# Down projection of a hybrid decoder layer: nine rooms for raw operands in place of five

## The chip, the cores and the metric

The kernel runs on one core of a Trainium2 chip. The metric is the device time of one execution in microseconds, as the median of several runs. Before the change it is 2085.34 us (three runs, 2084.3 to 2087.26). Smaller is better.

## The reference

One layer of a decoder trunk is computed for a prompt of 1024 tokens and for 8 single sampled tokens, 1032 columns in all, in float32. The layer has a gated delta rule, a sliding-window attention, an output projection and a gated feed-forward part with a short causal convolution; a final norm ends it. What matters here is its end:

```
h2 = _rmsnorm(x, lp['norm2_w']) * (1 + sc2) + sh2
gate = h2 @ lp['w_ffn_gate']
up = h2 @ lp['w_ffn_up']
...
gc = _causal_dwconv(gate_ext, lp['ffn_conv_w'], L) + lp['ffn_conv_b']
x = x + gt2 * ((jax.nn.silu(gc) * up) @ lp['w_ffn_down'])
```

The model width is 1024 and the hidden width D_FF is 2816, which is 22 tiles of 128 (`FT`).

## The kernel before

**Precision.** Each float32 operand is split in two parts, a high part that ACT (ScalarE) writes as a rounded copy and a low part that DVE (VectorE) forms as the difference (`split`, lines 127 to 130). A product is three matmuls, high by high, high by low and low by high (`mm3`, lines 178 to 182). So nearly all TensorE work carries line 180, 181 or 182, and all splits line 129 (ACT) and line 130 (DVE).

**Seven products for eight.** Gate, up and down each use a scheme of Winograd's kind: operands are cut in halves along two dimensions, sums and differences of the halves are formed, and seven half-size products give the four quarters of the result. Gate and up are computed for pairs of hidden tiles (`ffn_gate_up`, 11 passes); their weights are combined on POOL (GpSimd, line 1589) and split into tiles with the tags w0 to w6, of which w0 to w3 lie in the pool `pw`. At the end of each pass the seven combinations of the hidden activations go to a DRAM scratch, `xd` (lines 1718 to 1721): two directly, five after sums on POOL.

**The down projection** is `ffn_down`, from line 1726. Its seven products are called `i` = 5, 3, 4, 7, 1, 2, 6 in that order, grouped in chains `(5, 3)`, `(4, 7)`, `(1,)`, `(2,)`, `(6,)`. Each product sums over `G` = 11 tiles, so there are 77 steps `s`. A step has three stages:

- `fetch(s)` (line 1742) loads 128 columns by 512 of the weight on SP's DMA queue (line 1751) and 128 by 516 of activations from `xd` (line 1756) into one raw room of 1028 elements per partition. For the products 3, 4, 7, 1 and 6 the weight is a sum or difference of two blocks; the second block goes to a tile `ws` with three buffers (line 1754), and POOL combines the two (line 1755).
- `part(s)` (line 1759) splits the room: ACT writes the high half, DVE the low half, into an operand room. There are 13 operand rooms, taken in turn by the list `tags` (line 1730), so the operands of step s take the place of those of step s - 13. An `issue_after` keeps later splits behind certain instructions, among them `self.took`, the last copy of `take` (line 1763).
- `step(s, ...)` (line 1775) issues 24 matmuls, three for each of 8 PSUM banks: two column halves by four blocks of 128 output rows.

After a product's last step, `take` (line 1783) copies each of its 8 banks to SBUF on ACT (line 1786, tile `bml`). Inside a chain the next product goes on adding to the same banks, so its first matmul into a bank waits for that bank's copy. The copies are then added to the result by `add_gated` on DVE, two a step (lines 1472, 1476 and 1477). The last product, 6, is done bank by bank with the final norm between (`norm_rows`).

**The raw rooms before.** They are five, chosen by `s % 5`: for 0, 1 and 2 the tag `raw` of the pool `pw` (three buffers), for 3 and 4 the two halves of one tile with the tag `bmh0`, which was an operand of gate and up. A load into a room waits until the low half of the step five before has been formed, and for the two halves of `bmh0` until both steps before have been.

**What sets the order.** The program is written as a sequence of calls; a planner then orders each engine's instructions by priority (the order of the calls, as far as nothing else is said) and by when its own model of time holds them ready. On the chip each engine, and SP's queue of DMA issues, takes its list strictly in that order. In `ffn_down` the sequence is set by `fetch_to(n, split)` (line 1794). With `split` true it fetches and splits up to step n - 1, by turns. With `split` false, in the last six steps of each chain, it only fetches, up to a limit that keeps within the rooms, `done + 4 + (begun % 5 != 3)`. The main loop calls `fetch_to(s + 13, ...)` ahead of each step's matmuls, so the splits of up to 12 steps ahead come earlier in the sequence than those matmuls and than the copies of `take` that follow them.

Of the kernel before, what the change touches and what calls it, by code (L numbers as in the profile page):

```python
# [18 lines left out]
P = 128  # L19
# [45 lines left out]
class Step:  # L65
# [1660 lines left out]
    def ffn_down(self, pool, psum):  # L1726

        nc, I = self.nc, self.I
        G, n = FT // 2, NT // 2
# [8 lines left out]
        ready, loaded, waiting = {}, {}, ([], [])  # L1738
# [2 lines left out]

        def fetch(s):
            i, g = steps[s]
            if s % 5 == 3:
                ready["raw"] = self.t(self.bm, [P, KC, QW], "bmh0").rearrange("p k n -> p (k n)")
            raw = self.t(self.pw, [P, n + 512], "raw", bufs=3) if s % 5 < 3 else \
                ready["raw"][:, (s % 5 - 3) * 1040:(s % 5 - 3) * 1040 + n + 512]
            at, *src = made[i]
            src = [x if type(x) is not tuple else
                   I["w_ffn_down"][0][(2 * g + x[0]) * P:(2 * g + x[0] + 1) * P, 512 * x[1]:512 * x[1] + 512] for x in src]  # L1750
            nc.sync.dma_start(raw[:, n:], src[0])
            if len(src) > 1:
                other = self.t(self.pw, [P, 512], "ws", bufs=3)
                nc.sync.dma_start(other, src[1])
                nc.gpsimd.tensor_tensor(raw[:, n:], raw[:, n:], other, op=src[2])
            nc.sync.dma_start(raw[:, :n], self.xd[at, g])
            loaded[s] = raw

        def part(s):
            room = self.room(tags[s % len(tags)], [P, KC * QW])  # L1760
            hi, lo = room[:, :n + 512], room[:, n + 512:2 * (n + 512)]
            with ExitStack() as after:
                for ins in (self.last_up, self.last_copy) if 5 <= s < len(tags) else (self.took,) if s >= len(tags) and self.took else ():
                    after.enter_context(self.tc.issue_after(ins.ins))
                self.split(hi, lo, loaded.pop(s))
            ready[s] = hi, lo
            if s == 5:
                less.append(self.t(pool, [P, KC, 9], "less"))
                nc.gpsimd.tensor_scalar(less[0], self.mT[:, 40:48, :], -1.0, None, op0=ALU.mult)
                for j in (2, 3, 4):  # L1770
                    self.x1[j] = self.t(pool, [P, NT], f"x1_{j}")
            if 18 <= s < 24:
                nc.sync.dma_start(self.x1[s - 16], self.x1d[s - 16])
# [18 lines left out]
        s = begun = done = 0  # L1792

        def fetch_to(n, split=True):
            nonlocal begun, done
            n = min(n, len(steps))
            while done < n if split else begun < n and begun < done + 4 + (begun % 5 != 3):
                if begun == done or not split:
                    fetch(begun)
                    begun += 1  # L1800
                else:
                    part(done)
                    done += 1

        for c in chains[:-1]:
            ps = {(p, j): self.t(pl, [P, 512], tag, bufs=k)[:, :256 + 4 * p] for (p, j), (pl, tag, k) in zip(order, banks)}
            for i in c:
                for g in range(G):
                    fetch_to(s + len(tags), i != c[-1] or g < G - 6)
                    for p, j in order:  # L1810
                        step(s, ps[p, j], p, j, g == 0 and i == c[0], g == G - 1, {"skip_group_check": True} if i != c[0] else {})
                        if g == G - 1:
                            take(ps[p, j], i, p, j)
                    if g in range(2, 10):
                        for _ in range(2):
                            if waiting[0] or waiting[1]:
                                add(*(waiting[0] or waiting[1]).pop(0))
                    s += 1
        for x in waiting[0] + waiting[1]:
            add(*x)  # L1820
        fetch_to(len(steps))
        self.ffn_rows(pool, psum)
        tail = self.norm_rows(pool, psum, [2 * P, 3 * P])
# [248 lines left out]
```

## Time and profile before

| what | value |
|---|---|
| median of three runs | 2085.34 us (2084.3 to 2087.26) |
| span of the profiled execution | 2084.4 us (the page gives no other time for that execution) |
| mean granted TensorE clock | 0.991 of full speed |
| DVE busy | 1347.8 us (65%) |
| ACT busy | 900.2 us (43%) |
| POOL busy | 520.2 us (25%) |
| read from and written to HBM | 212.93 MB and 62.51 MB, 132 GB/s over the span |

How to read the profile: it is one execution. A page gives busy times by engine, then groups of instructions by line. The timeline lists instructions as start, duration, engine, line, operation, tiles written and read, shapes and count, and in brackets the idle time before and what ended it. The list of waits gives, for a pair of waiter and releaser, the sum, the number and the longest. The chain of waits follows what ended last back in time, step by step. A table by stretches of time gives the busy time of each engine with its number of instructions (PE, PEld, DVE, ACT, POOL), then the granted clock, the busy share of the 16 DMA engines and the GB/s moved. Matmuls overlap: a row's duration is over 0.2 us while they start 0.12 us apart. A few per cent of the matmul records are missing, so counts of matmuls are slightly low. Buffer numbers are left out of tile names: `pk`, `bml` and `bmh` each stand for several operand rooms, and `bmh` for the raw tile `bmh0` too.

### The profile page before, as it was taken

To read this page: it belongs to the slowest core of one execution; us is meant where nothing else is said; L and a number is where in the kernel's file an instruction comes from. 1 tells how busy PE (TensorE), PEld (TensorE's weight loads), DVE (VectorE), ACT (ScalarE), POOL (GpSimd) and SP (SyncE) were. 2 spreads that over 40 slices of the span, in tenths; PEclk is the share of its full clock that TensorE was granted. 3 is DMA by queue.
4 is the path that set the end of the run, shared out by engine and by line. 5 is a ranking of instruction groups with operands and counts; after the bars stand their busy time and mean duration, and the time that the engine had idled before them with its cause. 6 is when DMAs were issued, how large, how long until landed. Compare 5 with 4: busy or idle time off the path is not lost.

```text
span 2084.4 us, 41297 instructions
## 1 busy us (share of the span) xinstructions
PE 2012.7 (97%) x16245; PEld 1910.2 (92%) x16245; DVE 1347.8 (65%) x2714; ACT 900.2 (43%) x2233; POOL 520.2 (25%) x594
## 2 busy tenths in 40 slices
PE   7999998999999999989989999999999999999897
PEld 4987877799999999989989999999999999999897
DVE  5755768473655647656544675578876776767756
ACT  4664545433344243432342542354444444534443
POOL 2000000121321221201111000005575466446421
PEclk9999999999999999999999999999999999999999
DMA  8256443331332322312275855323333333488862
GB/s 300 62 144 210 135 167 116 117 94 51 80 80 61 73 72 52 89 42 62 63 223 172 285 186 163 112 63 97 105 91 112 102 92 112 136 305 266 291 215 94
DMA packets 301887, 275.75 MB, mean 132 GB/s; under 512 B 59730, under 2 KB 248111, under 8 KB 301676
## 3 DMA queue, kind: packets, MB, share of 16 engines
q1 hardware_dynamic: 295642, 252.14, 39.6%
q0 software_dynamic: 5552, 20.37, 2.8%
q8 instruction: 127, 2.08, 0.4%
q14 instruction: 68, 0.56, 0.1%
q10 hardware_dynamic: 498, 0.61, 0.1%
HBM read 212.93 MB, written 62.51 MB: 132 GB/s over the span
## 4 chain that ended last, share of the span: by engine, by line
PE 83%; DVE 5%; DMA 5%; ACT 3%; issue 1%; SPq 1%; POOL 1%; DVEq 0%; POOLq 0%; ACTq 0%
PE mm L180 19%; PE mm L181 18%; PE mm L182 18%; PE wv L180 3%; PE wv L182 3%; PE wv L181 3%; PE wy L182 2%; PE wy L180 2%; PE wy L181 2%; PE pv L652 1%; PE pt L190 1%; PE tp L190 1%; DVE x L1472 1%; PE mm L264 1%; PE rc L954 1%
## 5 line engine op out<-in xcount | busy, mean ns | idle before, releaser
L180 PE MATMUL mm<-b1h,wh 128*128 128x384 f32 (+1 forms) x1520 | 496.9, 328 | 3.7 <-ACT gt L1294 1.6
L181 PE MATMUL mm<-b1l,wh 128*128 128x384 f32 (+1 forms) x1520 | 489.3, 323 | 0.0
L182 PE MATMUL mm<-b1h,wl 128*128 128x384 f32 (+1 forms) x1520 | 488.0, 323 | 0.3 <-DVE wl L130 0.3
L180 PEld LDWEIGHTS mm<-b1h,wh 128*128 128x128 f32 x1520 | 286.7, 189 | 12.4 <-issue 4.6
L181 PEld LDWEIGHTS mm<-b1l,wh 128*128 128x128 f32 x1520 | 287.1, 189 | 4.4 <-issue 3.1
L182 PEld LDWEIGHTS mm<-b1h,wl 128*128 128x128 f32 x1520 | 286.3, 189 | 3.9 <-issue 2.8
L129 ACT ACTIVATE wh<-raw 128x1024 fp32r<-128x1024 f32 x83 | 87.0, 1049 | 122.4 <-PE mm L181 70.2
L130 DVE TENSOR_TENSOR wl<-raw,wh 128x1024 fp32r<-128x1024 f32 x82 | 101.0, 1233 | 57.2 <-ACT wh L129 55.1
L181 PE MATMUL mm<-pk,w 128*128 128x260 f32 (+1 forms) x440 | 124.8, 284 | 1.1 <-DVE pk L130 1.1
L180 PE MATMUL mm<-pk,w 128*128 128x260 f32 (+1 forms) x440 | 124.8, 284 | 0.0
L182 PE MATMUL mm<-pk,w 128*128 128x260 f32 (+1 forms) x440 | 124.5, 283 | 0.0
L130 DVE TENSOR_TENSOR w<-ws,w 128x512 fp32r<-128x512 f32 x88 | 78.0, 886 | 36.9 <-ACT w L129 36.7
L1626 ACT COPY bml<-mm 128x256 f32<-128x256 f32 (+1 forms) x132 | 48.9, 371 | 100.6 <-PE mm L182 96.7
L180 PE MATMUL mm<-bmh,w 128*128 128x260 f32 (+1 forms) x320 | 90.3, 282 | 0.0
L182 PE MATMUL mm<-bmh,w 128*128 128x260 f32 (+1 forms) x320 | 90.1, 282 | 0.0
L1681 DVE SCALAR_TENSOR_TENSOR fa<-fz,fcw,fa 128x512 f32<-128x512 f32 x88 | 75.2, 874 | 18.2 <-ACT fa L1679 17.9
L180 PE MATMUL mm<-b2h,wh 128*128 128x384 f32 (+1 forms) x256 | 83.2, 328 | 2.9 <-ACT wh L129 2.8
L181 PEld LDWEIGHTS mm<-pk,w 128*128 128x128 f32 x440 | 83.2, 189 | 1.3 <-DVE pk L130 1.3
L181 PE MATMUL mm<-b2l,wh 128*128 128x384 f32 (+1 forms) x256 | 83.6, 327 | 0.4 <-DVE b2l L130 0.4
L180 PEld LDWEIGHTS mm<-pk,w 128*128 128x128 f32 x440 | 83.2, 189 | 0.2 <-ACT bml L1626 0.2
L182 PEld LDWEIGHTS mm<-pk,w 128*128 128x128 f32 x440 | 83.4, 190 | 0.0
L182 PE MATMUL mm<-b2h,wl 128*128 128x384 f32 (+1 forms) x256 | 82.8, 326 | 0.0
(645 smaller groups left out, 5886.2 us busy)
## 6 DMA issues: line engine op xcount, KB each, us to landing
raw<-in_w_in_dram SPq DMA_DIRECT2D x59, 512.0 KB
ws<-in_w_ffn_down_dram SPq DMA_DIRECT2D x55, 256.0 KB
raw<-xd SPq DMA_DIRECT2D x47, 258.0 KB
raw<-in_w_ffn_down_dram SPq DMA_DIRECT2D x47, 256.0 KB
raw<-in_w_ffn_gate_dram SPq DMA_DIRECT2D x22, 512.0 KB
raw<-in_w_ffn_up_dram SPq DMA_DIRECT2D x22, 512.0 KB
qst<-in_w_mod_dram SPq DMA_DIRECT2D x16, 512.0 KB
raw<-in_w_mod_dram SPq DMA_DIRECT2D x16, 512.0 KB
```

Source lines behind the costliest of these rows:

```text
L129: self.nc.scalar.activation(hi, x, AF.Copy)
L130: (eng or self.nc.vector).tensor_tensor(lo, x, hi.bitcast(F32), op=ALU.subtract)
L180: mm(ps, whi, xhi, start=first, stop=False, **kw)
L181: mm(ps, whi, xlo, start=False, stop=False, **kw)
L182: self.last_mm = mm(ps, wlo, xhi, start=False, stop=last, **kw).ins
L190: self.nc.tensor.transpose(out, in_, self.ident[:p, :p])
L264: nc.tensor.matmul(ps[32 * j:32 * j + 32], self.cT[:, k0 + j, :], ws[j // 2][:, j % 2, :], start=k0 == 0, stop=k0 > 0)
L652: nc.tensor.matmul(pv[64 * r:64 * r + 64], V[:, n - back, ch], ps[:, r::2, :], start=back == 0, stop=back == (n > 0))
L954: yield step(nc.tensor.matmul(ds, kd[:, n, :], s, start=True, stop=True))
L1472: nc.vector.scalar_tensor_tensor(x[:, :np_], ps[:, :np_], by[:, j, 8:9], x[:, :np_], op0=ALU.mult, op1=ALU.add)
L1626: self.last_copy = nc.scalar.copy(r[p, i], x[p])
L1681: nc.vector.scalar_tensor_tensor(ai[:, c:e], zi[:, j + c:j + e], col(j), ai[:, c:e], op0=ALU.mult, op1=ALU.add)
```

## The change

The raw rooms are chosen by `s % 9`. For 0, 1 and 2 they are the three buffers of `raw`, for 3 and 4 the halves of `bmh0`, as before; for 5 to 8 they are the tiles w0 to w3 of `pw`, which held the split weights of gate and up and have one buffer each. Since a raw room has 1028 elements and a weight tile 1024, these four tiles grow by 4 elements per partition. The limit in `fetch_to` with `split` false is raised to suit. Nothing else is touched: the number of loads, splits, matmuls and copies and the 13 operand rooms are the same.

```
         def fetch(s):
             i, g = steps[s]
-            if s % 5 == 3:
+            if s % 9 == 3:
                 ready["raw"] = self.t(self.bm, [P, KC, QW], "bmh0").rearrange("p k n -> p (k n)")
-            raw = self.t(self.pw, [P, n + 512], "raw", bufs=3) if s % 5 < 3 else \
-                ready["raw"][:, (s % 5 - 3) * 1040:(s % 5 - 3) * 1040 + n + 512]
+            if s % 9 in (3, 4):
+                raw = ready["raw"][:, (s % 9 - 3) * 1040:(s % 9 - 3) * 1040 + n + 512]
+            elif s % 9 < 3:
+                raw = self.t(self.pw, [P, n + 512], "raw", bufs=3)
+            else:
+                raw = self.t(self.pw, [P, n + 512], f"w{s % 9 - 5}", bufs=1)
...
-            while done < n if split else begun < n and begun < done + 4 + (begun % 5 != 3):
+            while done < n if split else begun < n and begun < done + 8 + (begun % 9 != 3):
```

## The prediction

> **What bounds the kernel now.** I read the page first, then TensorE's waits from 1800 us on (the last gate/up product ends near 1836 us and the down projection follows), then the chain of waits around the one long wait, and last the timelines of the engines in that chain.
>
> ```profile
> span 2084.4 us, 41297 instructions
> ...
> PE 2012.7 (97%) x16245; PEld 1910.2 (92%) x16245; DVE 1347.8 (65%) x2714; ACT 900.2 (43%) x2233; POOL 520.2 (25%) x594
> ```
> ```profile
> PE mm L180 <- ACT bml L1786: 5.6, 1, 5.6
> PE wv L190 <- DVE x L1477: 1.0, 1, 1.0
> PE wy L190 <- ACT ws L1873: 1.0, 1, 1.0
> ```
>
> TensorE is busy 97% of the span, so the change can only pay where TensorE stands still or runs slowly. In the stage that the diff touches there is one such place: 5.6 us, waiting for a copy of line 1786, `take`. The other two are in the final norm. Seen from both queues:
>
> ```profile
> 1927.88 0.28 PE L182 MATMUL nr<-pk 128*128 128x260 f32 x1
> 1933.72 0.58 PE L180 MATMUL mm<-pk 128*128 128x256 f32 x1 [5.56 <-ACT bml L1786]
> ```
> ```profile
> 1924.42 1.06 ACT L129 ACTIVATE pk<-raw 128x1028 fp32r<-128x1028 f32 x1 [1.18 <-POOL raw L1755]
> 1926.65 1.07 ACT L129 ACTIVATE pk<-raw 128x1028 fp32r<-128x1028 f32 x1 [1.17 <-POOL raw L1755]
> 1928.87 1.06 ACT L129 ACTIVATE bmh<-bmh 128x1028 fp32r<-128x1028 f32 x1 [1.15 <-POOL bmh L1755]
> 1932.35 1.06 ACT L129 ACTIVATE bmh<-bmh 128x1028 fp32r<-128x1028 f32 x1 [2.42 <-POOL bmh L1755]
> 1933.32 0.35 ACT L1786 COPY bml<-mm 128x256 f32<-128x256 f32 x1
> ```
>
> Number the 77 steps of the down projection from 0 (11 for each product); step s is split on ACT as the s-th 128x1028 ACTIVATE. By that count the splits in the fence are those of steps 36 to 39, and TensorE has just ended step 32, the last of product 4. Product 7 adds onto the same PSUM banks, so step 33 must wait until `take` has copied each bank out. Bank 0 was complete one step before 1928, but ACT takes its queue in order, the planner put the split of step 39 ahead of the copies, and the data of step 39 came late. Why late:
>
> ```profile
> 1903.39 6.36 DVE x L1472 x8
> 1909.75 0.08 DVE x L1477
> 1909.83 0.08 DVE gtmp L1476
> 1909.90 0.10 DVE bml L130
> 1910.00 0.97 issue
> 1910.97 1.21 DVE bmh L130
> ...
> 1912.59 1.31 SPq L1756
> 1913.94 4.54 DMA bmh<-in_w_ffn_down_dram
> ...
> 1918.62 1.29 POOL bmh L1755
> 1919.93 1.08 ACT pk L129
> 1921.04 2.20 DVE pk L130
> ...
> 1925.10 5.37 DMA ws<-in_w_ffn_down_dram
> ...
> 1930.60 1.72 POOL bmh L1755
> ```
>
> This is a loop through five raw rooms, gone round twice: VectorE's low half frees a room, SP loads the step five later into it, GpSimd combines, ACT and VectorE split. It began with gated adds (line 1472) that held the low halves back until 1911. Meanwhile SP and the DMA engines had nothing to do:
>
> ```profile
> 1905.43 1.77 SPq L1754 DMA_DIRECT2D ws<-in_w_ffn_down_dram  x2
> 1912.21 0.33 SPq L1751 DMA_DIRECT2D bmh<-in_w_ffn_down_dram  x1
> ```
> ```profile
> 1902.00:1914.00 12.00, 12.00 (x103) 12.00 (x102) 12.00 (x21) 3.40 (x4) 4.42 (x3) 1.00 0.45 137
> 1832.00:1842.00 10.00, 10.00 (x86) 10.00 (x86) 7.98 (x9) 1.61 (x2) 8.82 (x10) 1.00 0.35 111
> 1874.00:1880.00 6.00, 6.00 (x53) 6.00 (x52) 5.87 (x7) 2.31 (x3) 4.70 (x3) 1.00 0.46 129
> 1920.00:1926.00 6.00, 6.00 (x53) 6.00 (x52) 5.87 (x4) 3.13 (x3) 4.32 (x3) 1.00 1.01 359
> 1926.00:1934.00 8.00, 2.44 (x20) 2.23 (x19) 5.67 (x4) 3.78 (x6) 5.07 (x4) 0.92 1.00 345
> 1934.00:1940.00 6.00, 6.00 (x30) 6.00 (x31) 5.97 (x7) 4.58 (x9) 3.80 (x3) 0.53 0.96 317
> ```
>
> The last three columns are granted clock, busy share of the DMA engines and GB/s. The share is 0.45 in the twelve microseconds ahead of the trouble and full during it: the loads came in a lump because the rooms did. The last row shows the second part of the loss: after the gap TensorE runs at a granted 0.53, 30 matmuls in 6 us where 53 went before, 23 fewer, which at 6/53 = 0.113 us each is 2.6 us.
>
> **The size of the loss.** Products without this trouble give the pace, by the first copy of `take` after each of products 7, 1 and 2:
>
> ```profile
> 1965.57 0.37 ACT L1786 COPY bml<-mm 128x256 f32<-128x256 f32 x1 [6.14 <-PE mm L182]
> ...
> 1997.01 0.37 ACT L1786 COPY bml<-mm 128x256 f32<-128x256 f32 x1 [11.33 <-PE mm L182]
> ...
> 2028.55 0.38 ACT L1786 COPY bml<-mm 128x256 f32<-128x256 f32 x1 [3.91 <-PE mm L182]
> ```
>
> (2028.55 - 1965.57) / 2 = 31.5 us for a product, 2.86 us for a step. The matmul that completes bank 0 at the end of product 3 is this one in the chain:
>
> ```profile
> 1894.06 0.14 PE mm L182
> ```
>
> From its end, 1894.2, to 1965.5 are 71.3 us for two products that should take 63.0. The loss is 8.3 us, which agrees with 5.6 + 2.6 = 8.2. That is all this stage can give back: 0.4% of the time.
>
> **The change part by part.** It adds and removes no instruction: the same 77 fetches, combinations and splits, and TensorE's work is untouched. Two things move.
>
> *The rooms.* Step 39 was loaded into the shared tile of steps 33 and 34, free at 1923.2 (the 1921.04 row and its 2.20). With nine rooms it takes the place of steps 30 and 31. The low half of step 31 is this row:
>
> ```profile
> 1913.48 1.21 DVE L130 TENSOR_TENSOR bml<-raw,bml 128x1028 fp32r<-128x1028 f32 x1
> ```
>
> So its room is free at 1914.7, 8.5 us earlier. The bytes come no sooner than the engines move them: steps 33 to 39 were loaded from 1912.2 on at nearly full share, and with four more rooms this can begin when SP now runs dry, 1905.4, that is 6.8 us earlier. The combination for step 39, which ended at 1930.60 + 1.72 = 1932.3, then ends at 1925.5, and its split at 1926.6. The copies follow, before TensorE ends step 32 at 1928.2. Both parts of the loss go. What is late next is VectorE, full in 1902 to 1914: but step 33's low half was ready near 1921, 7 us ahead of need, so its adds cost nothing while that lead lasts.
>
> *How far ahead the whole stage runs.* The idle DMA share of 1832 to 1842 (0.65 x 10 = 6.5 us) and of 1874 to 1880 (0.54 x 6 = 3.2 us) is also time in which rooms were full. Filled, it puts the loads up to 9.7 us further ahead. I count nothing for it, since TensorE does not wait there, but it decides the rivals.
>
> *The waits that are new.* Loads into w0 to w3 wait until the last up product has read its weights there, and all later loads stand behind them on SP. The first of these is step 5. From below the cost is nothing; from above, it holds step 5 until the up product's end, about 1836. This row is that step's split now:
>
> ```profile
> 1828.39 1.07 ACT L129 ACTIVATE bml<-raw 128x1028 fp32r<-128x1028 f32 x1
> ```
>
> Its matmuls come at the sixth step, about 1848. A load that lands 5.4 us after 1836, as the 1925.10 row did, and 1.07 + 1.21 us of split make 1843.7: 4 us are left. I take zero. The earlier loads could also press on the writing of the last hidden tile, but in 1832 to 1842 the engines are two thirds idle. The deeper `fetch_to` limit at a chain's end allows one load more or so, in stretches where TensorE has no wait: zero.
>
> Sum: 2085.34 - 8.3 = 2077.0 us. The profiled span is 2084.4, 0.9 us under the median of the runs; no other time of that execution is given, and I take the gain from the median.
>
> **The rivals.** All hang on one thing that the trace of before cannot show: where the planner puts the copies of step 32 among ACT's splits, now that by its own reckoning the loads are early too. It had put them behind split 39 when ACT had really reached 36, so it is more hopeful than the chip. The limit is split 44, since split 45 needs the operand room of step 32 itself. One more step's raw data are 256 + 256 + 258 KB, 0.79 MB, and at 317 to 359 GB/s they take 2.2 to 2.5 us; I use 2.4.
>
> *Part of the wait stays (0.14).* The copies stand behind split 40, ready at 1926.6 + 2.4 = 1929.0, or 41, at 1931.4: a gap of 1 to 3 us, a gain of 5 to 7, less up to 2.6 if the slow clock comes as well: 2078 to 2082. Whether it comes can be read from two earlier gaps:
>
> ```profile
> 1192.00:1195.00 3.00, 0.19 (x2) 0.00 (x0) 2.65 (x9) 3.00 (x9) 0.03 (x1) 1.00 1.06 386
> 1195.00:1199.00 4.00, 3.98 (x19) 3.98 (x20) 4.00 (x6) 2.88 (x4) 0.85 (x1) 0.57 1.05 400
> 1282.00:1285.00 3.00, 0.94 (x8) 0.72 (x7) 2.00 (x7) 1.58 (x5) 0.00 (x0) 1.00 0.47 124
> 1285.00:1289.00 4.00, 4.00 (x36) 4.00 (x35) 3.56 (x5) 2.07 (x3) 0.00 (x0) 1.00 0.83 250
> ```
>
> About 2.8 us idle brought the low clock, about 2.1 us did not. The Trainium skill, page "TensorE: Matmul & The Clock Gate", section "Why this matters for your kernels", asks only that gaps stay under about 3 us; by that rule no gap of this rival costs clock, and the 1192 row is against it.
>
> *Nothing changes (0.20).* The copies stand behind split 42, ready at 1926.6 + 3 x 2.4 = 1933.8, where they start now at 1933.3: 2085. The rows for it are the full shares of 1920 to 1934: rooms do not move bytes. The Trainium skill states the same of issuing, page "DMA: Bandwidth & Descriptors", section "Issuing engines are not separate DMA queues": all DMAs run on the same 16 engines, and more issuers save only issue time. By that reading alone, nothing is gained; the 0.45 share of 1902 to 1914 says that there were bytes to move earlier.
>
> *Slower (0.18).* The copies stand behind split 44, whose data come at 1926.6 + 5 x 2.4 = 1938.6. TensorE then stands 5.3 us longer than now: 2085.3 + 5.3 = 2090.6. This decides from split 43 on, and only if the loads ahead of 1902 have gained nothing. Against it: with the 9.7 us of idle share filled, split 44 is ready at 1928.9, and the wait is under 1 us. That is why I hold the full gain likelier than either.
>
> **How the numbers follow.** Full gain 0.48, a part 0.14, none 0.20, slower 0.18. The full gain alone spans 2074 to 2079: the runs shown lie from 1.0 us below to 1.9 us above their median, and with earlier data the two 1.0 us waits of the norm could go as well. About 0.2%, 4.2 us, is what a measurement here can tell. Half of the partial case is beyond it: faster 0.48 + 0.07 = 0.55, within 0.20 + 0.07 = 0.27, slower 0.18. The range goes from 2074 up to 2088, which takes in "nothing changes" with the highest run shown, and leaves the slower case out.
>
> **What would show it.** TensorE's list of waits after 1800 us without the 5.6 us row, and a granted clock of 1.00 through 1934 to 1940; the first copies after products 3 and 7 about 63 us apart; a DMA share well over 0.45 in the twelve microseconds after product 3, and over 0.35 in the ten from 1832; the copies of step 32 behind split 41 or earlier, or behind a later one whose data are there. The prediction is wrong if that wait stays with its data still on the way, if it turns up after another product, or if TensorE waits for the first steps' operands near 1840.

## The result: slower by 5.9 us

The changed kernel takes 2090.88 us, median of 21 runs (2084.77 to 2097.47), against 2085.01 us (21 runs, 2079.26 to 2093.31) for the kernel before. The ratio is 1.0028, with a 95% interval of 1.002 to 1.0036. The change costs 4 to 7.5 us where 8.3 us of gain were forecast. The profiled execution of the changed kernel took 2088.13 us with a span of 2086.4; a run's time lies 1.7 us over its span. A second set of ten runs (e8) came out 3.6 us over. TensorE's list of waits from 1790 us on, in the changed kernel:

```profile
PE mm L180 <- ACT pk L129: 5.2, 1, 5.2
PE mm L180 <- ACT bml L1790: 4.9, 1, 4.9
PE wy L190 <- ACT ws L1877: 1.0, 1, 1.0
```

The old wait for the copies (`take`, now line 1790) is still there, 4.9 us in place of 5.6. There is a new one of 5.2 us, for a split. One of the two 1.0 us waits of the norm is gone. Line 1790 is 1786 of before, 1759 is 1755 (the combination), 1758 is 1754 (the second operand's load) and 1760 is 1756 (the load of the hidden tile).

**The old wait.** ScalarE's timeline at the end of product 4 (start, duration, instruction, idle time ahead of it and its cause):

```profile
1928.76 1.07 ACT L129 ACTIVATE bmh<-bmh 128x1028 fp32r<-128x1028 f32 x1 [3.54 <-POOL bmh L1759]
1931.07 1.07 ACT L129 ACTIVATE bml<-bmh 128x1028 fp32r<-128x1028 f32 x1 [1.24 <-POOL bmh L1759]
1933.31 1.06 ACT L129 ACTIVATE bml<-w 128x1028 fp32r<-128x1028 f32 x1 [1.18 <-POOL w L1759]
1935.52 1.06 ACT L129 ACTIVATE bmh<-w 128x1028 fp32r<-128x1028 f32 x1 [1.14 <-POOL w L1759]
1937.72 1.06 ACT L129 ACTIVATE pk<-w 128x1028 fp32r<-128x1028 f32 x1 [1.15 <-POOL w L1759]
1938.69 0.35 ACT L1790 COPY bml<-mm 128x256 f32<-128x256 f32 x1
```

These are the splits of steps 39 to 43. The first copy of step 32 stood behind split 39 before and stands behind split 43 here. The rooms let the planner count on later steps' data, and it put four more splits ahead of the copies.

**The new wait.** ScalarE's timeline at the end of product 5, and SyncE's a little earlier:

```profile
1865.34 1.06 ACT L129 ACTIVATE pk<-raw 128x1028 fp32r<-128x1028 f32 x1 [4.24 <-DMA raw<-xd]
1869.01 0.37 ACT L1790 COPY bml<-mm 128x256 f32<-128x256 f32 x1 [2.61 <-PE mm L182]
```
```profile
1859.26 0.33 SPq L1760 DMA_DIRECT2D w<-xd  x1
1860.01 0.33 SPq L1760 DMA_DIRECT2D raw<-xd  x1
```

The split at 1865.34 is that of step 10, the last of product 5 and the one that reads the last hidden tile. Its load is the issue at 1860.01, behind those of steps up to 25; in the kernel before only steps up to 14 and a part of step 15 stood ahead of it, and its split ran at 1854.96. SyncE's order is one part of the delay: with the later loads put behind it (e2) the load goes 19.6 us after the end of the gate/up products, here 24.7, before about 13. The other part is that the hidden sums themselves were late. GpSimd's timeline of before, then of after, over the last sums of line 1718:

```profile
1835.48 0.73 POOL L1718 TENSOR_TENSOR r<-fa 128x256 f32<-128x256 f32 x1
1836.58 1.67 POOL L1718 TENSOR_TENSOR r<-fa,fa 128x260 f32<-128x260 f32 x1 [0.37 <-DVE fa L1703]
1838.21 1.73 POOL L1718 TENSOR_TENSOR r<-fa 128x260 f32<-128x260 f32 x1
1839.88 1.75 POOL L1721 DMA_DIRECT2D xd<-r  x2
```
```profile
1835.96 2.27 POOL L1759 TENSOR_TENSOR bmh<-bmh,ws 128x512 f32<-128x512 f32 x1
1838.19 1.72 POOL L1718 TENSOR_TENSOR r<-fa,fa 128x256 f32<-128x256 f32 x1
...
1843.27 1.73 POOL L1718 TENSOR_TENSOR r<-fa 128x260 f32<-128x260 f32 x1
1844.96 0.87 POOL L1721 DMA_DIRECT2D xd<-r  x1
1845.85 1.39 POOL L1759 TENSOR_TENSOR w<-w,ws 128x512 f32<-128x512 f32 x1
1847.19 0.88 POOL L1721 DMA_DIRECT2D xd<-r  x1
```

The raw operands of later steps are in their rooms so early that four combinations were put ahead of the last write: one ahead of the sums, two among them, one between the two writes. All four later sums take 1.72 to 1.74 us, where before the first two of these took 0.74. Both writes were out by 1841.63 before (1839.88 + 1.75) and are by 1848.07 here (1847.19 + 0.88).

**Where the time went.** The gate/up products end at 1836.4 us before and 1835.3 after. Counted from there, to about 0.3 us, this is when the first copy after a product starts, and when the program ends, in every run's profile (us; "waits" are TensorE's at steps 10 or 11 and at step 33):

| kernel | after product 5 | 4 | 7 | 2 | end | end less product 2 | waits |
|---|---|---|---|---|---|---|---|
| before | 26.4 | 96.9 | 129.2 | 192.1 | 248.0 | 55.9 | 0, 5.6 |
| after | 33.7 | 103.4 | 135.8 | 198.8 | 251.1 | 52.3 | 5.2, 4.9 |
| e8, after again | 34.1 | 103.3 | 134.2 | 197.2 | 249.5 | 52.3 | 5.6, 4.6 |
| e1 | 26.4 | 97.6 | 129.9 | 192.9 | 245.2 | 52.3 | 0, 6.2 |
| e2 | 34.0 | 103.3 | 134.3 | 196.0 | 249.4 | 53.4 | 5.4, 3.0 |
| e3 | 29.9 | 98.0 | 129.9 | 192.9 | 245.2 | 52.3 | 1.4, 4.6 |
| e4 | 34.4 | 97.0 | 128.5 | 191.5 | 243.8 | 52.3 | 6.1, 0 |
| e5 | 26.4 | 93.3 | 124.2 | 185.9 | 241.3 | 55.4 | 0, 1.9 |
| e6 | 26.4 | 91.8 | 121.4 | 184.5 | 236.8 | 52.3 | 0, 0.4 |
| e7 | 26.4 | 96.5 | 127.4 | 190.5 | 242.8 | 52.3 | 0, 5.2 |
| e9 | 26.4 | 100.3 | 131.5 | 194.5 | 246.8 | 52.3 | 0, 8.6 |
| e10 | 26.4 | 96.5 | 127.7 | 190.8 | 245.7 | 54.9 | 0, 5.2 |
| e11 | 26.4 | 92.3 | 122.0 | 185.0 | 237.4 | 52.4 | 0, 0.7 |
| e12, e6 again | 26.4 | 92.6 | 122.2 | 185.3 | 237.6 | 52.3 | 0, 1.2 |

The changed kernel loses 7.3 us at step 10 (33.7 - 26.4: the wait and the half clock behind it), wins 0.7 by product 7 (135.8 - 129.2 = 6.6) and 3.6 at the end (52.3 against 55.9): 251.1 - 248.0 = 3.1 us slower in these two executions. Its median is 5.9 us over. Where the rest comes from is not shown. The timed runs of the changed kernel had a lower granted clock (a mean of 0.9880 over the 21 runs, 0.9904 over the 35 runs of the kernel before that went with e1 to e4), but so had its profiled execution (0.988 against 0.991), whose span is only 2.0 us longer. Since the length of the part ahead of the down projection varies from one execution to the next (the gate/up products ended between 1833.9 and 1843.2 us in the fourteen profiles), the table is the sharper comparison of edits, and the ratios are the verdict.

### The profile page after: what moved, and what is told of

It is laid out like the page before. It is cut to its first block, busy times and chain, and to the rows that moved or that the text cites. A ratio compares the mean times of both kernels' runs of the same rounds, so it can differ in the third digit from the quotient of the medians.

```text
span 2086.4 us, 41279 instructions
## 1 busy us (share of the span) xinstructions
PE 2014.0 (97%) x16245; PEld 1911.2 (92%) x16245; DVE 1350.6 (65%) x2714; ACT 899.2 (43%) x2233; POOL 528.9 (25%) x594
## 4 chain that ended last, share of the span: by engine, by line
PE 80%; DVE 7%; DMA 6%; ACT 3%; issue 2%; SPq 1%; POOL 0%; DVEq 0%; POOLq 0%; ACTq 0%
PE mm L180 18%; PE mm L181 18%; PE mm L182 18%; PE wv L180 2%; PE wv L182 2%; PE wv L181 2%; PE wy L180 1%; PE wy L182 1%; PE wy L181 1%; PE pv L652 1%; DMA raw<-in_w_swa_out_dram 1%; DVE pk L130 1%; PE pt L190 1%; PE tp L190 1%; PE mm L264 1%
## 5 line engine op out<-in xcount | busy, mean ns | idle before, releaser
L130 DVE TENSOR_TENSOR wl<-raw,wh 128x1024 fp32r<-128x1024 f32 x82 | 102.4, 1250 | 60.1 <-ACT wh L129 58.7
```

The costliest lines, as they stand in the source:

```text
L130: (eng or self.nc.vector).tensor_tensor(lo, x, hi.bitcast(F32), op=ALU.subtract)
```

## The experiments

The first theory was that the order of the queues, not the movement of bytes, decides: combinations and loads pulled ahead of step 10's data at the start, copies behind more splits at step 33. The rival was that four more loads under way at once slow the data.

**e1: the combinations behind the last writing of the sums.**

```diff
-        nc.gpsimd.dma_start(self.xd[0:5, g, :, c // 2:c // 2 + n].rearrange("i p n -> p i n"), sums)
+        self.xd_out = nc.gpsimd.dma_start(self.xd[0:5, g, :, c // 2:c // 2 + n].rearrange("i p n -> p i n"), sums)
...
-                nc.gpsimd.tensor_tensor(raw[:, n:], raw[:, n:], other, op=src[2])
+                with self.tc.issue_after(self.xd_out.ins):
+                    nc.gpsimd.tensor_tensor(raw[:, n:], raw[:, n:], other, op=src[2])
```

> Nine rooms; the only edit is that GpSimd's combinations for the down projection stand behind its last writing of the hidden sums. Theory 1 (the order of the queues at the start: the early loads let combinations go ahead of the last sums on GpSimd, and loads of steps up to 25 go ahead of step 10's on SyncE): the sums take 0.74 us each again and are written from about 1840 us, not 1845; step 10's load stands behind step 19's in place of step 25's and is issued near 1852, not 1860; TensorE's 5.2 us wait at step 10 goes (under 1 us) with the half clock behind it, and the copies after product 5 start near 1862, not 1869. The wait after step 32 stays (the planner has the copies behind split 40), 3 to 5 us. Time: the changed kernel less 7.9, plus up to 4.6 that the tail takes back: 2 us below to 3 above the kernel before. Rival (the bytes of four more loads under way at once hold step 10's data): the wait at step 10 stays above 4 us and the time stays at the changed kernel's, about 6 above the kernel before.

Measured: 2083.21 us (11 runs), ratio 0.9991 (0.9981 to 1.0001). GpSimd's timeline has the order and the durations of before, and TensorE's waits have lost the one at step 10:

```profile
1839.01 0.73 POOL L1718 TENSOR_TENSOR r<-fa 128x256 f32<-128x256 f32 x1
...
1843.42 1.75 POOL L1721 DMA_DIRECT2D xd<-r  x2
1845.19 1.30 POOL L1760 TENSOR_TENSOR raw<-raw,ws 128x512 f32<-128x512 f32 x1
```
```profile
PE mm L180 <- ACT bml L1791: 6.2, 1, 6.2
PE wy L190 <- ACT ws L1878: 1.0, 1, 1.0
```

Four more rooms are in use here and step 10 does not wait, so the rival is out for this wait. This one order was the whole new loss. The wait at step 33 stayed and was longer than expected (6.2 for 3 to 5): seven copies stand behind split 40.

**e2: the loads of steps 15 and later behind step 10's load.** GpSimd's order is that of the changed kernel.

```diff
-            nc.sync.dma_start(raw[:, n:], src[0])
+            with self.tc.issue_after(ready["last"].ins) if s >= 15 else nullcontext():
+                nc.sync.dma_start(raw[:, n:], src[0])
...
+            if s == 10:
+                ready["last"] = x
```

The two other loads of `fetch` are wrapped in the same way.

> Nine rooms; the only edit is that SyncE's loads of steps 15 and later stand behind step 10's load. GpSimd's order is the changed kernel's (four combinations among the last sums). Theory 1: the sums still end near 1845 and are written to memory by 1854; step 10's load is issued then, not at 1860, lands 4 to 5 us later, and its split ends near 1860.5, so that TensorE waits 0 to 1.5 us at step 10. With TensorE earlier by 6 us the planner puts the copies of step 32 behind split 39, and that wait is 0 to 3 us. Time: 8 to 0 us below the kernel before. Rival (bytes under way): the load of step 10 is issued earlier but takes over 8 us, TensorE waits above 4 us at step 10, time about 6 above the kernel before. If both waits here and in the run with the combinations behind the sums go, either queue alone was enough to cause the delay, or enough to cure it.

Measured: 2091.52 us (12 runs), ratio 1.0028 (1.0013 to 1.0043). Step 10 did not wait: its load was issued at 1856.67 and its split ran at 1859.35. But the wait came back one step later, and the time is 6 us over the kernel before, where 0 to 8 under it were expected. ScalarE's timeline:

```profile
1859.35 1.07 ACT L129 ACTIVATE pk<-raw 128x1028 fp32r<-128x1028 f32 x1 [7.59 <-DMA raw<-xd]
1862.91 1.06 ACT L129 ACTIVATE bml<-w 128x1028 fp32r<-128x1028 f32 x1 [2.50 <-POOL w L1761]
...
1870.11 1.06 ACT L129 ACTIVATE bml<-raw 128x1028 fp32r<-128x1028 f32 x1 [1.15 <-POOL raw L1761]
1871.08 0.35 ACT L1795 COPY bml<-mm 128x256 f32<-128x256 f32 x1
```

SyncE stood at step 10's load, which had to wait for the late sums, and held the loads behind it. The copies of step 10 had been planned behind split 18, whose data came late by that, and step 11 waited 5.4 us for them. A wait of 1.5 us for a low half is new too, within product 4. It is the mechanism of step 33 at another product: whatever delays the splits delays the copies planned behind them.

**e3: both orders.** Both edits together.

> Nine rooms with both edits (combinations behind the last sums' writing, loads of steps 15 and later behind step 10's). Theory 1: step 10's load is issued near 1849 as in the kernel before; no wait at step 10. The planner has the copies of step 32 behind split 40 here, so 2 to 5 us of wait stay there. Time: 4 below to 2 above the kernel before. Rival (bytes): wait at step 10 above 4 us, 6 above the kernel before.

Measured: 2084.51 us (11 runs), ratio 1.0001 (0.9991 to 1.001). As expected at step 10 and at step 33 (4.6 us); the copies of step 10 stand behind splits 19 and 20 and cost 1.4 us, which was not expected. The second edit adds nothing to the first.

**e4: the copies of step 32 behind split 38, nine rooms.** The kernel stops splitting in the last six steps of the other products; this does so in product 4 too.

```diff
-                    fetch_to(s + len(tags), i != c[-1] or g < G - 6)
+                    fetch_to(s + len(tags), i not in (c[-1], 4) or g < G - 6)
```

> Nine rooms; the only edit is that in the last six steps of product 4 nothing more is split, as the kernel does at the end of the other products, so that all eight copies of step 32 stand behind split 38 in place of splits 42 and 43. Theory 1: the 4.9 us wait at step 33 and the half clock after it go (under 1 us); the 5.2 us wait at step 10 stays. Time: the changed kernel less 7.5, plus up to 4.6 in the tail: 1.6 below to 3 above the kernel before. Rival (the wait at step 33 is by late data, not by the place of the copies): the wait moves to the operands of a step between 33 and 40 with 3 us or more, and the time stays at the changed kernel's.

Measured: 2083.49 us (11 runs), ratio 0.999 (0.998 to 1.0). The wait at step 33 is gone, and none took its place; the copies wait for TensorE now, not the other way round:

```profile
1929.99 1.07 ACT L129 ACTIVATE bmh<-raw 128x1028 fp32r<-128x1028 f32 x1 [2.40 <-POOL raw L1759]
1937.39 0.38 ACT L1790 COPY bml<-mm 128x256 f32<-128x256 f32 x1 [6.34 <-PE mm L182]
```

**e5: the same edit on the kernel before, five rooms.**

> Five rooms as before; the only edit is that nothing more is split in the last six steps of product 4, so that all eight copies of step 32 stand behind split 38 in place of splits 39 and 40. From the end of the gate/up products to the program's end the kernel before takes 248.0 us, of which 8.3 are the wait at step 33 and the half clock behind it. Theory 1 (what costs is the place of the copies in ScalarE's queue, not the number of rooms): the wait goes, the copies after product 4 start near 89 us after the gate/up end (before: 96.9), the stage takes about 239.7 us, the time is about 8 us under the kernel before (2077). Rival (the recorded prediction's reading: the data of step 39 and later come too late with five rooms): the wait reappears at the operands of a step of product 7, 3 us or more, and the time is 0 to 4 us under the kernel before.

Measured: 2080.43 us (12 runs), ratio 0.9975 (0.9964 to 0.9985). This is the recorded prediction's gain, in part, without any room: 6.7 us in the table (248.0 - 241.3), 5.2 by the ratio, where about 8 were expected. Of the wait 1.9 us is left, since split 38 is late as well (it ran at 1926.23, with TensorE ready at 1925.7).

**e7: five rooms for steps 0 to 19, nine from step 20.** This undoes the change at the start alone, and it is the recorded prediction's mechanism by itself. The room is chosen by `k` in place of `s % 5`, and the limit of `fetch_to` follows it.

The edit is shown against the kernel before, and so are those of e9 and e10.

```diff
-            if s % 5 == 3:
+            m, k = (5, s % 5) if s < 20 else (9, (s - 20) % 9)
+            if k == 3:
```

> Five rooms for steps 0 to 19, nine from step 20 on: the start is that of the kernel before (copies after product 5 at 26.4 us after the gate/up end, no wait at step 10), and the planner has six copies of step 32 behind split 39 and two behind split 40. This is the recorded prediction's mechanism by itself. By it the data of step 39 are there about 7 us earlier and the wait at step 33 is under 1 us; with the shorter end of the nine-room runs (52.3 against 55.9) the time is 10 to 12 us under the kernel before. Rival (by bytes and VectorE's order the data of step 39 are no earlier with more rooms): the wait stays at 4 to 6 us, and only the end gains: 3 to 4 us under the kernel before.

Measured: 2082.62 us (11 runs), ratio 0.9985 (0.9975 to 0.9996). The rival is right: the wait is 5.2 us, though the copies stand behind splits 39 and 40 as in the kernel before. SyncE's timeline, from the load at which it had stood since 1910, and GpSimd's combinations of steps 38 and 39:

```profile
1916.44 0.33 SPq L1756 DMA_DIRECT2D w<-in_w_ffn_down_dram  x1
...
1917.38 0.38 SPq L1759 DMA_DIRECT2D ws<-in_w_ffn_down_dram  x1
...
1919.28 0.38 SPq L1756 DMA_DIRECT2D raw<-in_w_ffn_down_dram  x1
...
1920.19 0.42 SPq L1761 DMA_DIRECT2D raw<-xd  x1
...
1928.48 0.33 SPq L1759 DMA_DIRECT2D ws<-in_w_ffn_down_dram  x1
```
```profile
1930.85 1.28 POOL L1760 TENSOR_TENSOR raw<-raw,ws 128x512 f32<-128x512 f32 x1
1933.96 1.64 POOL L1760 TENSOR_TENSOR raw<-raw,ws 128x512 f32<-128x512 f32 x1 [1.83 <-DMA ws<-in_w_ffn_down_dram]
```

The first two rows are the weights of step 37 and the second operand of step 34. Step 39's weights and hidden tile were asked for at 1919.28 and 1920.19. Its second operand, which the combination needs too, was asked for at 1928.48. The second operands have three rooms of their own, which the change leaves at three: step 39's takes that of step 36, whose combination had ended at 1927.4, when SyncE had later steps' raw loads to issue first. Counted from the gate/up end, the raw load went from 87.7 us (before) to 79.2, the second operand's only from 88.7 to 88.4, and the combination's end from 95.9 to 95.5.

**e8: the changed kernel again.**

> The changed kernel once more, unedited, for a second profile of it: how far its two waits vary between executions. Theory 1 (planned orders decide, and they are fixed): the waits stand at the same two places, behind the same instructions, 4 to 6.5 us each, and the time is about 6 us over the kernel before. Rival (chance meetings of transfers): one of the waits is under 2 us or at another step.

Measured: 2089.0 us (10 runs), ratio 1.0017 (1.0004 to 1.0029), that is 3.6 us over the kernel before, where about 6 were expected. The waits stand at the same steps in this second profile, 5.6 and 4.6 us, as fixed orders would have it and not chance.

**e9: seven raw rooms and five for second operands, from step 20.** Of the four empty rooms two hold raw operands and two second operands.

```diff
-                other = self.t(self.pw, [P, 512], "ws", bufs=3)
+                m = (s - 20) % 5 if s >= 20 else 0
+                other = self.t(self.pw, [P, 512], "ws", bufs=3) if m < 3 else \
+                    self.t(self.pw, [P, n + 512], f"w{m - 3 + 2}", bufs=1)[:, :512]
```

> Five raw rooms to step 19 as in the late-nine run; from step 20 on seven raw rooms, and the other two of the four empty rooms hold second operands, so that these have five rooms in place of three. In the late-nine run the second operand of step 39 was asked for at 88.4 us after the gate/up end, right when the combination of step 36 had freed its room, though the raw room had been loaded since 79. Theory 2 (the three rooms of the second operands hold the data of step 39, not the raw rooms): the second operand of step 39 is asked for 3 us or more earlier, and its combination ends by 92.5 (late-nine: 95.5; before: 95.9). The planner has all copies behind split 42 here, whose combination then ends near 97 to 99 (before 101.5), so that 3 to 6 us of the wait at step 33 can stay all the same; time 3 to 8 us under the kernel before. Rival (the DMA engines are full, bytes decide): the combination of step 39 ends at 95 or later, the wait is 7 us or more, and the time is the kernel before's or above.

Measured: 2087.89 us (12 runs), ratio 1.0001 (0.9989 to 1.0013). The second operand of step 39 was asked for at 82.6 us, 5.8 earlier, as theory 2 has it; its combination ended at 92.7, 2.8 earlier, so the theory was right in kind and holds for half of the size. What came next is GpSimd itself:

```profile
1927.74 2.28 POOL L1762 TENSOR_TENSOR w<-w,w 128x512 f32<-128x512 f32 x1
1929.99 2.24 POOL L1762 TENSOR_TENSOR w<-w,ws 128x512 f32<-128x512 f32 x1
1932.20 4.45 POOL L1762 TENSOR_TENSOR raw<-raw,ws 128x512 f32<-128x512 f32 x2
```

The combinations stand end to end at 2.2 us each, and the planner has the copies behind split 42: step 33 waits 8.6 us, more than in any other run, though its data are earlier than in any run above. The price by the place of the copies was underestimated (3 to 6 expected), and the time is that of the kernel before, not 3 to 8 us under it.

**e10: five raw rooms and seven for second operands, from step 20.** As e9, with all four rooms for second operands:

```diff
-                other = self.t(self.pw, [P, 512], "ws", bufs=3)
+                m = (s - 20) % 7 if s >= 20 else 0
+                other = self.t(self.pw, [P, 512], "ws", bufs=3) if m < 3 else \
+                    self.t(self.pw, [P, n + 512], f"w{m - 3 + 0}", bufs=1)[:, :512]
```

> Five raw rooms throughout, and from step 20 on all four empty rooms hold second operands (seven rooms for them). The planner has the copies of step 32 behind splits 40 (two) and 41 (six). Theory 2 says that both kinds of room hold these loads in turn: with five raw rooms the loads of steps 37 and later still wait for VectorE's low halves, which the gated adds hold back to 1911, so the combination of step 39 ends within 2 us of before's 95.9, and the wait at step 33 stays at 4 to 7 us. Time within 4 us of the kernel before. If instead the combination ends 3 us or more earlier and the wait falls under 2 us, the raw rooms had no part in it.

Measured: 2087.4 us (12 runs), ratio 1.0006 (0.9996 to 1.0017). The combination of step 39 ended at 93.3 (2.6 earlier than before, where up to 2 were expected), and the wait stayed at 5.2. Neither kind of room alone brings the data 6.8 us forward, nor do both.

**e6 and e12: nine rooms with the edits of e1 and e4, run twice.**

> Nine rooms, with the combinations behind the last sums' writing and the copies of step 32 behind split 38. Theory 1: both waits go, the copies after the six products start near 26, 58, 89, 121, 152 and 184 us after the gate/up end, and the rest takes 52.3 us as in every nine-room run so far (before: 55.9): stage 236 us, time about 12 us under the kernel before (2074). Rival (more rooms shift the loss on: each wait cured brings the next one, by bytes): a wait of 3 us or more turns up at another step, and the time is 2078 or above.

> The run with nine rooms and both cures once more, for its time: stage 236.8 us after the gate/up end in its first profile, against 248.0 before. Theory 1: again 236 to 238, waits under 1 us at steps 10 and 33, time 8 to 12 us under the kernel before. Rival (the first profile was a lucky one): a wait of 2 us or more, time less than 6 us under it.

Measured: e6 has ratio 0.9963 (0.9948 to 0.9978; six runs from 2072.47 to 2081.75, a seventh of 6823.93 left out), e12 2076.65 us (6 runs) with ratio 0.9945 (0.9926 to 0.9963). The wait at step 10 goes; of the one at step 33, 0.4 us (e6) and 1.2 us (e12) are left. e12's list is nearly what the prediction hoped to see of the change:

```profile
PE mm L180 <- ACT bml L1791: 1.2, 1, 1.2
PE wy L190 <- ACT ws L1878: 1.0, 1, 1.0
```

**e11: seven and five rooms from step 20 (the diff of e9), with the edit of e4.**

> The run with seven raw rooms and five for second operands from step 20 on, with the copies of step 32 put behind split 38 as well. Theory 1: no wait at step 10 (start as before), no wait at step 33; copies after the six products at 26, 58, 89, 121, 152, 184 us after the gate/up end, the end 52.3: stage 236 to 238 us, time 10 to 12 us under the kernel before. Rival (more data under way early brings a new wait): a wait of over 2 us at another step, stage over 240.

Measured: 2076.03 us (6 runs), ratio 0.9944 (0.9927 to 0.9961). By the ratios it is 12 us under the kernel before, e12 11 and e6, the same kernel as e12, 8; they are not told apart.

## Why the prediction was wrong

**The size of the loss: right.** Putting the copies elsewhere (e4) takes the loss at step 33 away without moving a room, and the ideal of 31.5 us for a product holds.

**The rooms: the step that failed for the gain.** "So its room is free at 1914.7, 8.5 us earlier" came out in e7, where step 39's raw load goes 8.5 us earlier (87.7 to 79.2), though there it takes another room than the prediction reckoned with. In the changed kernel it goes 2.0 us earlier (85.7). The next sentence failed, that "with four more rooms this can begin when SP now runs dry, 1905.4, that is 6.8 us earlier", and that the combination ends so much sooner. The four more rooms had been filled by then, and the next raw load waited, as before, for a low half that stood behind VectorE's gated adds. In the changed kernel, SyncE's queue, the low half, and the stretch after product 3:

```profile
1898.98 9.58 SPq L1758 DMA_DIRECT2D ws<-in_w_ffn_down_dram  x6
1914.80 0.33 SPq L1755 DMA_DIRECT2D raw<-in_w_ffn_down_dram  x1
```
```profile
1913.56 1.22 DVE L130 TENSOR_TENSOR bml<-raw,bml 128x1028 fp32r<-128x1028 f32 x1
```
```profile
1901.00:1913.00 12.00, 12.00 (x103) 12.00 (x103) 12.00 (x18) 10.82 (x15) 7.63 (x6) 1.00 0.38 132
```

The load at 1914.80 is step 37's; the room is that of step 28, whose low half is the second row shown. In e7 it is the same load, 1916.44. Counted from the gate/up end, 1905.4 is 69.0 us. The raw load at which SyncE stood came at 75.8 us before (step 33), at 76.3 in e7 and at 79.5 in the changed kernel. The DMA share of those twelve microseconds, which was to be "well over 0.45", is 0.38, and 0.33 in e7 (1905.7 to 1917.7). So the prediction's words on VectorE, "its adds cost nothing while that lead lasts", went wrong as well: the adds set when the rooms came free.

The combination of step 39 ends 0.4 us sooner in e7, and 2.5 in the changed kernel (93.4 against 95.9). In e7 the second operand came last. The critical chain quoted in the prediction pointed at it: its last transfer, `1925.10 5.37 DMA ws`, goes into a second operand's room, of which there are three and which the change does not add to. SyncE's order adds to it: step 34's second operand went at 1917.38, behind step 37's raw load, though its room had been free since step 31's combination ended at 1911.2. This is read from the rows; no run changed that order alone. In the changed kernel the raw load came last, with the second operand asked for at 81.8. I called the loop one "through five raw rooms". It was two loops side by side, with a third limit, GpSimd's 2.2 us for a combination, behind them (e9).

**The place of the copies: the rivals' mechanism, and it came true.** The prediction made all hang on it and held the full gain likelier, because earlier data would outrun the planner. The changed kernel has the copies behind splits 43 and 44, and their data were not earlier by enough: split 43 starts at 102.4 us, before at 104.0. The first copy so starts 6.5 us later than before (103.4 against 96.9), near the 5.3 us of the rival "slower". TensorE waits only 4.9 us for it because it came to step 33 late itself, after the 7.3 us lost at step 10; that the wait looks like "nothing changes" is luck. What this place of the copies costs with TensorE on time no run shows; e9 and e1, with the copies elsewhere, have waits of 8.6 and 6.2 us.

**The waits that are new: the step that failed for the sign.** The load into the empty rooms was rightly costed at zero: step 5's, the first, was issued at 1817.4, and those of steps 6 to 8 by 1824.1, all ahead of the up product's end, and step 5's split ran at 1827.27 (1828.39 before). But "The earlier loads could also press on the writing of the last hidden tile, but in 1832 to 1842 the engines are two thirds idle" looked only at the DMA engines. The press came on GpSimd, whose queue holds both the sums and the combinations, and on SyncE's order: 7.3 us at step 10, all of it taken back by one line of order (e1). No rival named it; the slower one stood at step 33. The prediction did name the place where it would show, "TensorE waits for the first steps' operands near 1840"; it came at 1861.

**The norm: right as a possibility.** "With earlier data the two 1.0 us waits of the norm could go as well": with nine or seven raw rooms the end takes 52.3 us (53.4 in e2) for 55.9, with five 54.9 to 55.9. These 2.6 to 3.6 us are the one thing that the rooms alone gave.

The sum would have been + 7.3 at step 10, - 0.7 at step 33, - 3.6 in the norm: + 3.0, against 3.1 in the profiles. The further 2 to 3 us of the medians (5.9 against 3.1, and 3.6 against 1.5 in e8) stay open.

## What to carry to other kernels

Before adding rooms, list every kind of room that a step's data pass through, and look at the last transfer of the critical chain: the room it lands in is a limit too. Where a planner orders in-order queues, more rooms let it pull later work ahead, so look at what else stands in each of those queues, and pin what must come first. Here the edit that places the copies and the edit that places the combinations, together with the rooms, took the kernel 8 to 11 us under the one before; the first of them, without the rooms, took it 5 under; the rooms alone cost 4 to 6.

## What the runs showed of the hardware

Two-operand additions on GpSimd and on VectorE that run side by side stretch each other. GpSimd's sums take 0.74 us, and 1.72 beside VectorE's low halves; its combination takes 1.30, and 2.2 beside them. VectorE's timeline in e9 shows the other side. The first low half began 0.08 us ahead of a combination and took 1.23 us, while that combination took 2.28 (the row at 1927.74 above); the next ones began while a combination ran:

```profile
1927.66 1.23 DVE L130 TENSOR_TENSOR pk<-bmh,pk 128x1028 fp32r<-128x1028 f32 x1 [2.29 <-ACT pk L129]
1928.91 2.20 DVE L130 TENSOR_TENSOR bmh<-bmh,bmh 128x1028 fp32r<-128x1028 f32 x1
1931.15 2.17 DVE L130 TENSOR_TENSOR bmh<-w,bmh 128x1028 fp32r<-128x1028 f32 x1
```

The two seem to take turns: 1.30 + 1.23 is 2.5, and the pair goes by in 2.2. The Trainium skill, page "SBUF — State Buffer", section "Who interferes with whom", says that a VectorE instruction with two SBUF inputs and a GpSimd one that reads SBUF exclude each other, and these rows agree with it to within the 0.3 us that overlap.

The half clock came in pieces of 3.4 us, and the length of a gap did not settle how many: gaps of 5.2 us at step 33 brought 3.4 us (e7 and e10), 4.6 us brought 6.8 (e3) and 3.4 (e8), 8.6 us brought 10.2 (e9), and gaps of 3.0 (e2) and 1.9 us (e5) none, though the gap of 2.8 us in the prediction's rows did bring it. At step 33 the half clock begins 0.1 us or more ahead of the gap's end, so 3 to 6 us of it fall on work that then takes twice its time: a gap of about 5 us costs itself and 1.5 to 3 us more.
